# One paced stream of modulation sums, shorter inversion steps, and an earlier start of the z jobs, in a one-layer hybrid block

## The chip, the cores and the metric

The kernel runs on one core of a Trainium2 chip. The metric is the device time of one execution in microseconds (us). Three executions of the kernel before took 1974.28, 1973.03 and 1969.95 us; the median is 1973.03.

## What is computed

One layer for one batch of T = 256 tokens with D = 2048 channels, everything in float32:

```python
mod = silu(c) @ W_ada + b_ada      # 6 x 2048 numbers: shift/scale/gate for the mixer and for the FFN
h = rms_norm(x) * (1 + scale_m) + shift_m
proj = h @ W_in                    # mLSTM q,k,v,o and gates; GDN q,k,v, z, beta, decay; merge gates
y_a = (sigmoid(a_o) * norm(bidirectional mLSTM, 4 heads)) @ W_a
o_b = bidirectional gated delta rule, 16 heads, chunks of 64
      # each chunk: T = inverse(I + beta * k k^T * decay, strictly lower), u = T (beta v), w = T (beta exp(g) k)
y_b = (norm(o_b) * silu(z)) @ W_b
x = x + gate_m * ((g_a * y_a + g_b * y_b) @ W_out)
x = x + gate_f * (silu(gate) * up) @ W_down      # FFN of width 5632 on the normed, modulated x
return rms_norm(x)
```

## The kernel before

**Matmuls.** Every large product is made in split precision: a raw weight tile (1 MB) is loaded on SP's DMA queue into `raw`, ScalarE (ACT) copies half of it into the high part `wh` (line 213, or 182 for the narrow jobs), VectorE (DVE) subtracts to get the low part `wl` (line 215, or 184), and TensorE (PE) makes three products: high times high, high times low, low times high (lines 234 to 236). `raw`, `wh` and `wl` have three buffers each. Half a raw tile is a *half chunk*: 12 matmuls of 512 columns in `tjob`, 24 of 256 columns in `fjob`. A job of `tjob` is 8 half chunks for 512 output columns. The loop body makes the split of a half chunk and then its matmuls; with the argument `early` = n, the first n splits are made at the first `next` of the job, before its PSUM tiles are taken, and all splits of the job keep the written order (`order`). What is not given to `order` is placed by a scheduler that may move it among its neighbours on the same engine.

**Stages.** The projections of x with the modulation's first two parts come first, then the gated delta rule (GDN) in four groups of four heads, g = 0 to 3; then `y_b`, mLSTM, `y_a`, the output jobs `o`, and the FFN (gate, up, down), which takes from about 1260 us to the end. In the GDN stage the chain of small steps leaves TensorE free, so a stock of filling jobs `rest` (the mLSTM projections v, o, a and the merge gates mb, ma) is run between them: `fill(n)` runs n half chunks of the first job in `fills`.

**One GDN group.** `invert(g)` runs `gdn_invert(g)`, which inverts the 64 small triangles of the group's chunks by 30 rank-one updates on VectorE, two instructions each (the `utmp` and `uu` operations, line 704 on). It begins after a load of the triangles from DRAM (`uu` from `inst_d`). It yields whenever the size of the updates since the last yield is over 720, and at each yield `invert` runs one half chunk. Ahead of it, `invert` runs 4 half chunks (6 for g = 0). The inverted blocks go through DRAM and come back in `gdn_blocks(g)`; `fill(8)` stands between its first two steps. Then the loop over two pairs of heads, p = 0 and 1, with n = 1 to 9, interleaves three things: the steps of `gdn_phase2(g, p)` (matmuls p1 to p4, pa, pb, pc, po, then the norm, the transposes px), the next group's narrow jobs `b` and their heads' `gdn_phase1` (through `stream`), and fills. In `gdn_phase1` the products `ks` are turned into the tiles mi, mb, gg and at by ten VectorE operations and a transpose. At the end of groups 0 to 2 the next group's z job (`z_job(g + 1)`, 8 half chunks) is put in front of the fills, and `invert(g + 1)` runs. In group 3 two mLSTM heads (`first2`) are started beside the GDN.

**Modulation sums.** Parts 2, 3 and 4 of the modulation (48 vectors of 128), and part 5 in the FFN, are not made on TensorE. For each vector `ask()` loads 1 MB of W_ada on SP's queue, and `add()` multiplies it by silu(c) and sums it in one VectorE instruction (line 124, 2.28 us each). `pump()` is called once per half chunk and paces them: `every` says after how many half chunks a sum is owed, `held` forbids a sum, `age` counts half chunks since the load was asked. `room` holds the pool, the tag, the number of buffers and the number of loads asked at once.

```python
elif asked:
    if owed[0] and age[0] > 2 and not held[0]:
        owed[0] = 0
        add()
elif unasked and every[0]:
    ask()
```

The pace before: `every` is 1 in the loop over p and n; it is 0 in the inversions and in the z jobs, and from the end of group 3 to the end of the first mLSTM heads; it is 1 again for mLSTM heads 2 and 3; for the `y_a` jobs `room` is changed to three buffers of the pool "sr" and `every` is 4; in the `o` jobs `sums()` is called at fixed places, and `sums(P)` finishes all that are left at step 4 of the last one.

Of the kernel before, what the change touches and what calls it, by code (L numbers as in the profile page):

```python
# [9 lines left out]
F32 = mybir.dt.float32  # L10
# [5 lines left out]
P = 128  # L16
T = 256
D = 2048
# [34 lines left out]
def hybrid_block(ctx: ExitStack, tc: tile.TileContext, xr, nfr, crow, pk_d, cst_d, ada2, ada4, win0, winb, wint, wba, wbb, wo, wgu, wd, out, dbg=None):  # L53
# [3 lines left out]
    def pool(stack, name, bufs=1, **kw):  # L57
        return stack.enter_context(tc.tile_pool(name=name, bufs=bufs, **kw))
# [3 lines left out]
    rows_p = pool(ctx, "rows")  # L62
# [9 lines left out]
    def order(ins, yes=True):  # L72

        return tc.keep_in_program_order(ins) if yes else ins
# [30 lines left out]
        order(S.activation(row_c[:, g * 512 : (g + 1) * 512], pc_, AF.Silu))  # L105


    room = [(rows_p, "ada", 1, 1)]
    asked, unasked, age = [], [], [0]

    def ask():

        pl, tag, bufs, _ = room[0]
        part, b = unasked.pop(0)
        raw = pl.tile([P, D], F32, tag=tag, bufs=bufs, name=f"ada{part}_{b}")
        order(nc.sync.dma_start(raw, ada4[part - 2, b]))
        asked.append((part, b, raw))
        age[0] = 0

    def add():  # L120

        part, b, raw = asked.pop(0)
        c = part * KB + b
        order(V.scalar_tensor_tensor(raw, raw, 1.0, row_c[:, :D], ALU.mult, ALU.mult, accum_out=mod[:, c : c + 1]))  # L124
        if b == KB - 1:
            c = slice(part * KB, part * KB + KB)
            V.tensor_tensor(mod[:, c], mod[:, c], pk[:, PK_ADAB + c.start : PK_ADAB + c.stop], ALU.add)
# [16 lines left out]
            f()  # L144

    count, every = [0], [0]
    owed, held = [0], [False]

    def sums(n=1):

        while n and (unasked or asked):
            while unasked and len(asked) < room[0][3]:
                ask()
            add()
            n -= 1

    def pump():
        count[0] += 1
        age[0] += 1
        if every[0] and count[0] % every[0] == 0:  # L160
            owed[0] = 1
        if room[0][3] > 1:
            if owed[0]:
                owed[0] = 0
                sums()
        elif asked:
            if owed[0] and age[0] > 2 and not held[0]:
                owed[0] = 0
                add()
        elif unasked and every[0]:  # L170
            ask()

    def fjob(name, src, done):
# [93 lines left out]
    fills = []  # L267

    def fill(n=1):

        while n and fills:
            if next(fills[0], None):
                n -= 1
            else:
                fills.pop(0)
# [90 lines left out]
    def z_job(g, early=0):  # L366
        def done(ps):
            szs[g] = evp.tile([P, 2, 512], F32, tag="sz", bufs=1, name=f"sz{g}")
            for t in range(2):
                S.activation(szs[g][:, t], ps[t], AF.Silu)  # L370
        return tjob(f"z{g}", [wint[g, u] for u in range(4)], hh, hl, done, early)
# [121 lines left out]
    with ExitStack() as s0:  # L493
# [18 lines left out]
        def loads(b):  # L512
            ra = [w0.tile([P, D + 2], F32, tag="ra", bufs=5, name=f"ra{b}_{i}") for i in range(2)]
            raw = st.tile([P, N0, P], F32, tag="raw", bufs=3, name=f"raw0_{b}")
            for i in range(2):
                order(nc.sync.dma_start(ra[i], ada2[b, :, i]))
            order(nc.sync.dma_start(raw, win0[b]))
            return ra, raw
# [10 lines left out]
        ra, raw = loads(0)  # L529
# [18 lines left out]
        for b in range(KB):  # L548
            if b:
                ra, raw = loads(b)  # L550
# [15 lines left out]
        zj = z_job(0, 3)  # L566
# [121 lines left out]
    def gdn_invert(g):  # L688

        uu = uus.pop(g)  # L690
        tmp = bk.tile([64, 256], F32, tag="utmp", bufs=1, name=f"utmp{g}")
        inv = inv_d[g].rearrange("j b (x h) i -> h (b x) j i", h=GRP)

        def store(rows):
            for e in range(GRP):
                G.dma_start(inv[e, :, rows], uu[16 * e : 16 * e + 16, rows])

        yield
        order(V.memset(uu.rearrange("p j i -> p (j i)")[:, ::33], 1.0))
        size = 0  # L700
        for i in range(30, 0, -1):
            w = 31 - i
            t3 = tmp[:, 0 : i * w].rearrange("p (j c) -> p j c", j=i)
            order(V.tensor_tensor(
                t3,
                uu[:, 0:i, i : i + 1].broadcast_to([64, i, w]),
                uu[:, i : i + 1, i + 1 :].broadcast_to([64, i, w]),
                ALU.mult,
            ))
            order(V.tensor_tensor(uu[:, 0:i, i + 1 :], uu[:, 0:i, i + 1 :], t3, ALU.add))  # L710
            if i == 16:
                store(slice(16, 32))
            size += i * w + 125
            if size > 720:
                size = 0
                yield
        store(slice(0, 16))
# [165 lines left out]
    def drive(gen, n=2):  # L883
        for _ in gen:
            fill(n)
# [132 lines left out]
    def invert(g):  # L1018
        gen = gdn_invert(g)
        next(gen)  # L1020
        fill(4 if g else 6)
        for _ in gen:
            fill(1)

    invert(0)
    for g in range(4):
        blocks = gdn_blocks(g)
        next(blocks)
        fill(8)
        next(blocks)  # L1030
        fill(1)
        pairs = [gdn_phase2(g, p) for p in range(2)]
        if g == 3:
            settle()
            sf.close()
            mq["pool"] = pool(sq_, "mq", side="right")
            first2 = [mlstm(h) for h in range(2)]
            for c in first2:
                next(c)
        every[0] = 1  # L1040
        for p in range(2):
            pieces = stream(4 * g + 2 * p + 4)
            for n in range(1, 10):

                held[0] = n < 4
                if p == 0:
                    next(blocks, None)
                next(pairs[p], None)
                if g == 3 and n == (8, 4)[p]:
                    next(first2[p])  # L1050
                for _ in range(last[n] if g == 3 else second[n] if p else after[n]):
                    next(pieces)
            for _ in pairs[p]:
                pass

            if g < 3:
                while 4 * g + 2 * p + 5 not in heads:
                    next(pieces)
        if g < 3:
            fills.insert(0, z_job(g + 1))  # L1060
            every[0] = owed[0] = 0
            invert(g + 1)
    settle()
    sx.close()
# [53 lines left out]
            yield from y_b(g)  # L1118

    o4s = [o_load(g) for g in range(2)]  # L1120
    every[0] = owed[0] = 0
    cores = steps(*first2)
    fill(1)
    next(cores)
# [19 lines left out]
    o_split(3, o4s[3])  # L1144
    fill(2)
    drive(cores, 3)
    every[0] = 1
    drive(steps(mlstm(2), mlstm(3)), 3)
    fill(1000)
    mgh, mgl = big(bigC, F32R, "mgh"), big(bigC, F32R, "mgl")  # L1150
    sm_.close()
    sr_ = ExitStack()
    if asked:
        add()
    room[0] = (pool(sr_, "sr"), "sr", 3, 3)
    gm = room[0][0].tile([P, D], F32, name="gm")
    dgs = {}

    def row_diag(part, g, rp):
        ms = mods[:, part == 5]  # L1160
        if not g:
            m = mod[:, part * KB : (part + 1) * KB]
            V.tensor_copy(ms[:, 0], m)
            V.tensor_tensor(ms[:, 1], m, ms[:, 0].bitcast(F32), ALU.subtract)
        dg = dgs[part, g] = rp.tile([P, 2, 4, P], F32R, tag="dg", bufs=2, name=f"dg{part}_{g}")
        for i in range(2):
            V.tensor_tensor(
                dg[:, i], ident.unsqueeze(1).broadcast_to([P, 4, P]),
                ms[:, i, 4 * g : 4 * g + 4].bitcast(F32).unsqueeze(2).broadcast_to([P, 4, P]), ALU.mult,
            )  # L1170
# [6 lines left out]
            PE.matmul(pr, onesr, woven(dg[:, i]), start=i == 0, stop=i == 1)  # L1177
        S.activation(woven(dst[:, g * 512 : (g + 1) * 512]), pr.rearrange("p (c h) -> p c h", h=2), AF.Copy)

    every[0] = 4  # L1180
    for g in range(4):
        for i, _ in enumerate(y_a(g)):
            if g and i == 3:
                merged(g - 1, mgh, mgl)
            if i in (1, 5) and g < 2:
                row_diag(2, 2 * g + i // 4, room[0][0])
            if i in (3, 7) and g < 2:
                row_spread(2, 2 * g + i // 4, gm)
    every[0] = 0


    def o_job(g, front=None):
# [26 lines left out]
    def root():  # L1219

        order(S.activation(rs1[:, 2:3], ones1, AF.Sqrt))
# [83 lines left out]
    for g in range(4):  # L1305
        if g == 3:
            root()
        for i, _ in enumerate(o_job(g, front_o if g == 3 else None) if g else o_first, 0 if g else 2):
            if i in ((4, 7), (2, 5), (2, 5), (0, 2))[g]:
                sums()  # L1310
            if g == 3 and i == 4:
                sums(P)
                V.scalar_tensor_tensor(
                    affn, mod[:, 4 * KB : 5 * KB], 1.0, pk[:, PK_NFFN : PK_NFFN + KB], ALU.add, ALU.mult
                )
    if dbg is not None and "x1" in dbg:
        G.dma_start(dbg["x1"], x1)
    room[0] = (rows_p, "ada", 1, 1)
    ada_parts(5)
    sw.close()  # L1320
    sr_.close()
# [73 lines left out]
    for j in range(FB // 4):  # L1395
# [4 lines left out]
        for e2 in range(2):  # L1400
            px = gps(f"pxf{j}_{e2}")
            for e in range(2):
                f = 2 * e2 + e
                for t in range(2):
                    PE.transpose(px[:, e * T + t * P : e * T + (t + 1) * P], sg[:, t, f * P : (f + 1) * P], ident)
            b = 4 * j + 2 * e2
# [156 lines left out]
```

## Time and profile before

| | |
|---|---|
| runs | 1974.28, 1973.03, 1969.95 us; median 1973.03 |
| profiled execution | 1974.3 us; span from first to last instruction 1972.4 us |
| mean granted TensorE clock | 0.994 |
| busy | PE 98%, weight loads (PEld) 86%, DVE 71%, ACT 52%, POOL 6% |
| memory | 467.07 MB read, 16.82 MB written, 245 GB/s over the span |

Everything in the profile belongs to one execution. "Busy" is the share of the span in which the engine ran an instruction; PE and PEld overlap. "PEclk" is the granted TensorE clock, 1.00 at full speed. In a list of operations each line has the start (us from the start of the span), the duration in us, the engine, the line of the kernel, the operation, the tiles out<-in with their shapes, and, in brackets, the wait before it and what ended it.

### The profile page before, as it was taken

To read this page: it belongs to the slowest core of one execution; us is meant where nothing else is said; L and a number is where in the kernel's file an instruction comes from. 1 tells how busy PE (TensorE), PEld (TensorE's weight loads), DVE (VectorE), ACT (ScalarE), POOL (GpSimd) and SP (SyncE) were. 2 spreads that over 40 slices of the span, in tenths; PEclk is the share of its full clock that TensorE was granted. 3 is DMA by queue.
4 is the path that set the end of the run, shared out by engine and by line. 5 is a ranking of instruction groups with operands and counts; after the bars stand their busy time and mean duration, and the time that the engine had idled before them with its cause. 6 is when DMAs were issued, how large, how long until landed. Compare 5 with 4: busy or idle time off the path is not lost.

```text
span 1972.4 us, 27079 instructions
## 1 busy us (share of the span) xinstructions
PE 1929.4 (98%) x10418; PEld 1703.5 (86%) x10418; DVE 1405.5 (71%) x2067; ACT 1030.0 (52%) x1555; POOL 116.5 (6%) x211
## 2 busy tenths in 40 slices
PE   8999999999999999999999999999999999999998
PEld 6878889998998899889787888888888888888886
DVE  6779887887888798866577878866665665555554
ACT  3137656764766577565544444644444444444444
POOL 0001210111001010110100000200000000000000
PEclk9999999999999999999999999999999999999999
DMA  9987676766566666586777888566676665565663
GB/s 399 420 349 226 184 249 240 252 214 208 203 217 213 237 218 229 192 296 246 277 282 266 323 317 330 191 252 238 238 265 241 237 238 205 197 213 197 208 199 142
DMA packets 78962, 485.64 MB, mean 246 GB/s; under 512 B 10585, under 2 KB 15969, under 8 KB 24433
## 3 DMA queue, kind: packets, MB, share of 16 engines
q1 hardware_dynamic: 63216, 450.69, 62.9%
q0 software_dynamic: 8160, 17.88, 4.5%
q10 hardware_dynamic: 7458, 15.36, 2.1%
q8 instruction: 81, 1.33, 0.3%
q14 instruction: 47, 0.39, 0.1%
HBM read 467.07 MB, written 16.82 MB: 245 GB/s over the span
## 4 chain that ended last, share of the span: by engine, by line
PE 81%; DVE 8%; DMA 6%; ACT 2%; issue 1%; POOL 0%; ACTq 0%; SPq 0%; DVEq 0%; POOLq 0%
PE acc_gt L234 4%; PE acc_gt L235 4%; PE acc_gt L236 4%; PE acc_up L236 4%; PE acc_up L235 4%; PE acc_up L234 4%; PE acc_d L236 4%; PE acc_d L235 4%; PE acc_d L234 4%; DMA ra<-ada 3%; PE acc_b L187 2%; PE acc_b L188 2%; PE acc_b L189 2%; PE acc_o L236 2%; PE acc_o L234 2%; PE acc_o L235 2%
## 5 line engine op out<-in xcount | busy, mean ns | idle before, releaser
L215 DVE TENSOR_TENSOR wl_d<-raw_d,wh_d 128x1024 fp32r<-128x1024 f32 x88 | 107.7, 1224 | 105.9 <-ACT wh_d L213 105.9
L215 DVE TENSOR_TENSOR wl_up<-raw_up,wh_up 128x1024 fp32r<-128x1024 f32 x88 | 107.7, 1224 | 100.2 <-ACT wh_up L213 100.1
L215 DVE TENSOR_TENSOR wl_gt<-raw_gt,wh_gt 128x1024 fp32r<-128x1024 f32 x88 | 108.1, 1229 | 80.2 <-ACT wh_gt L213 80.2
L187 PE MATMUL acc_b<-hh,wh_b 128*128 128x256 f32 x576 | 163.0, 283 | 0.6 <-ACT wh_b L182 0.6
L189 PE MATMUL acc_b<-hh,wl_b 128*128 128x256 f32 x576 | 159.6, 277 | 0.8 <-DVE wl_b L184 0.8
L188 PE MATMUL acc_b<-hl,wh_b 128*128 128x256 f32 x576 | 159.2, 276 | 0.0
L213 ACT ACTIVATE wh_d<-raw_d 128x1024 fp32r<-128x1024 f32 x88 | 92.9, 1056 | 126.5 <-PE acc_d L235 117.7
L213 ACT ACTIVATE wh_gt<-raw_gt 128x1024 fp32r<-128x1024 f32 x88 | 92.9, 1056 | 118.6 <-PE acc_gt L235 71.1
L213 ACT ACTIVATE wh_up<-raw_up 128x1024 fp32r<-128x1024 f32 x88 | 92.8, 1055 | 108.1 <-PE acc_up L235 77.1
L124 DVE SCALAR_TENSOR_TENSOR ada<-ada,crow 128x2048 f32<-128x2048 f32 x64 | 146.0, 2284 | 0.0
L234 PE MATMUL acc_gt<-wh_gt,hfh 128*128 128x512 f32 x352 | 135.6, 385 | 0.6 <-ACT hfh L1350 0.6
L235 PE MATMUL acc_gt<-wh_gt,hfl 128*128 128x512 f32 x352 | 134.9, 383 | 0.0
L236 PE MATMUL acc_gt<-wl_gt,hfh 128*128 128x512 f32 x352 | 134.1, 381 | 0.0
L234 PE MATMUL acc_up<-wh_up,hfh 128*128 128x512 f32 x352 | 133.4, 379 | 0.0
L235 PE MATMUL acc_up<-wh_up,hfl 128*128 128x512 f32 x352 | 133.4, 379 | 0.0
L236 PE MATMUL acc_up<-wl_up,hfh 128*128 128x512 f32 x352 | 133.4, 379 | 0.0
L234 PE MATMUL acc_d<-wh_d,ffh 128*128 128x512 f32 x344 | 130.5, 379 | 0.0
L235 PE MATMUL acc_d<-wh_d,ffl 128*128 128x512 f32 x344 | 130.5, 379 | 0.0
L236 PE MATMUL acc_d<-wl_d,ffh 128*128 128x512 f32 x344 | 130.4, 379 | 0.0
L561 PE MATMUL first<-x,raw 128*128 128x256 f32 x512 | 114.5, 382 | 7.2 <-ACT x L555 7.2
L561 PEld LDWEIGHTS first<-x,raw 128*128 128x128 f32 x512 | 96.0, 190 | 25.7 <-ACT x L555 13.3
L189 PEld LDWEIGHTS acc_b<-hh,wl_b 128*128 128x128 f32 x576 | 111.3, 193 | 1.0 <-DVE wl_b L184 1.0
(383 smaller groups left out, 5263.1 us busy)
## 6 DMA issues: line engine op xcount, KB each, us to landing
ada<-ada SPq DMA_DIRECT2D x64, 1024.0 KB, 6.0
raw_gt<-wgu SPq DMA_DIRECT2D x44, 1024.0 KB, 4.9
raw_up<-wgu SPq DMA_DIRECT2D x44, 1024.0 KB, 4.9
raw_d<-wd SPq DMA_DIRECT2D x44, 1024.0 KB, 4.9
raw_b<-winb SPq DMA_DIRECT2D x36, 1024.0 KB, 5.3
ra<-ada SPq DMA_DIRECT2D x32, 1025.0 KB, 15.8
raw<-win SPq DMA_DIRECT2D x16, 1024.0 KB, 14.5
raw_z<-wint SPq DMA_DIRECT2D x16, 1024.0 KB, 5.0
```

The costliest lines, as they stand in the source:

```text
L124: order(V.scalar_tensor_tensor(raw, raw, 1.0, row_c[:, :D], ALU.mult, ALU.mult, accum_out=mod[:, c : c + 1]))
L187: PE.matmul(o, wh[:, k], woven(hh[:, kk]), start=kk == 0, stop=False)
L188: PE.matmul(o, wh[:, k], woven(hl[:, kk]), start=False, stop=False)
L189: PE.matmul(o, wl[:, k], woven(hh[:, kk]), start=False, stop=kk == KB - 1)
L213: order(S.activation(wh, raws[u][:, k0 : k0 + 2], AF.Copy), early)
L215: order(V.tensor_tensor(wl, raws[u][:, k0 : k0 + 2], wh.bitcast(F32), ALU.subtract), early)
L234: order(PE.matmul(ps[t], xh[:, kk, c], woven(wh[:, k]), start=kk == 0, stop=False), early and steps > 1)
L235: PE.matmul(ps[t], xl[:, kk, c], woven(wh[:, k]), start=False, stop=False)
L236: PE.matmul(ps[t], xh[:, kk, c], woven(wl[:, k]), start=False, stop=kk == last)
L561: PE.matmul(first[o], raw[:, o], x[:, b], start=b == 0 and o % 2 == 0, stop=b == KB - 1 and o % 2 == 1)
```

## The change

- `room` goes: a sum always has the one buffer "ada", so one load is under way at a time, from the GDN stage to the FFN.
- A new bound `calm`: a new load is asked for only when `age` has reached it. It is 1 at first, 3 in the loop over p and n of groups 0 to 2, and 1 again from the inversion on. `age` is set to 0 by `ask` and now also by a sum.
- `every` is set to 1 once per group, right after the first step of `gdn_blocks(g)` and so ahead of `fill(8)`, and stays 1 through `y_b`, mLSTM, `y_a` and `o`, until step 3 of the last `o` job, where `sums(P)` now stands. In `invert(1)` to `invert(3)` it is 0 as before. The fixed `sums()` calls in the `o` jobs go, and so does the pace of 4 in `y_a`.
- `gdn_invert` yields when the size is over 580 instead of 720: 13 yields in the updates instead of 10, and one half chunk is run at each.
- The z job of group g + 1 is created with `early` = 1 at p = 1, n = 9, and its first split is made there, ahead of that step of `gdn_phase2` and of what is left of the stream; the same job is then put in front of the fills.

The FFN and the amount of work are unchanged.

```diff
-    room = [(rows_p, "ada", 1, 1)]
...
     def ask():
-        pl, tag, bufs, _ = room[0]
         part, b = unasked.pop(0)
-        raw = pl.tile([P, D], F32, tag=tag, bufs=bufs, name=f"ada{part}_{b}")
+        raw = rows_p.tile([P, D], F32, tag="ada", name=f"ada{part}_{b}")
...
-    owed, held = [0], [False]
+    owed, held, calm = [0], [False], [1]
     def sums(n=1):
         while n and (unasked or asked):
-            while unasked and len(asked) < room[0][3]:
+            if not asked:
                 ask()
...
     def pump():
...
-        if room[0][3] > 1:
-            if owed[0]:
-                owed[0] = 0
-                sums()
-        elif asked:
+        if asked:
             if owed[0] and age[0] > 2 and not held[0]:
-                owed[0] = 0
+                owed[0] = age[0] = 0
                 add()
-        elif unasked and every[0]:
+        elif unasked and every[0] and age[0] >= calm[0]:
             ask()
...
-            if size > 720:
+            if size > 580:
                 size = 0
                 yield
...
         next(blocks)
+        every[0], held[0] = 1, False
         fill(8)
...
-        every[0] = 1
+        calm[0] = 3 if g < 3 else 1
         for p in range(2):
...
                     next(blocks, None)
+                if g < 3 and p and n == 9:
+                    zj = z_job(g + 1, 1)
+                    next(zj)
                 next(pairs[p], None)
...
-            fills.insert(0, z_job(g + 1))
+            fills.insert(0, zj)
             every[0] = owed[0] = 0
+            calm[0] = 1
             invert(g + 1)
...
-    every[0] = owed[0] = 0
+    held[0] = False
     cores = steps(*first2)
...
-    every[0] = 1
     drive(steps(mlstm(2), mlstm(3)), 3)
...
-    if asked:
-        add()
-    room[0] = (pool(sr_, "sr"), "sr", 3, 3)
-    gm = room[0][0].tile([P, D], F32, name="gm")
+    sr = pool(sr_, "sr")
+    gm = sr.tile([P, D], F32, name="gm")
...
-    every[0] = 4
     for g in range(4):
         for i, _ in enumerate(y_a(g)):
...
-    every[0] = 0
...
         for i, _ in enumerate(o_job(g, front_o if g == 3 else None) if g else o_first, 0 if g else 2):
-            if i in ((4, 7), (2, 5), (2, 5), (0, 2))[g]:
-                sums()
-            if g == 3 and i == 4:
+            if g == 3 and i == 3:
+                every[0] = owed[0] = 0
                 sums(P)
```

More of the change, by code (lines that the diff above doesn't have):

```diff
@@ L1185, in hybrid_block @@
             if i in (1, 5) and g < 2:
-                row_diag(2, 2 * g + i // 4, room[0][0])
+                row_diag(2, 2 * g + i // 4, sr)
             if i in (3, 7) and g < 2:
                 row_spread(2, 2 * g + i // 4, gm)
-    every[0] = 0
     def o_job(g, front=None):
@@ L1317, in hybrid_block @@
         G.dma_start(dbg["x1"], x1)
-    room[0] = (rows_p, "ada", 1, 1)
     ada_parts(5)
```

## The prediction, made before the change was run

> **What bounds the kernel now.** I read the page first, then who TensorE waited for, then busy time by stretch, then the timeline at the places that the change moves.
>
> ```profile
> span 1972.4 us, 27079 instructions
> PE 1929.4 (98%) x10418; PEld 1703.5 (86%) x10418; DVE 1405.5 (71%) x2067; ACT 1030.0 (52%) x1555; POOL 116.5 (6%) x211
> ```
>
> TensorE (PE) is busy for 1929.4 of 1972.4 us. The change leaves every matmul in place, so all that it can win or lose is in the 43 us of idle time and in the clock. Who ended that idle time:
>
> ```profile
> engine line waited for: us in total, times, longest us
> PE acc_ya L236 <- DVE wl_ya L215: 3.8, 2, 2.2
> PE acc_z L234 <- ACT wh_z L213: 2.5, 1, 2.5
> PE p L770 <- DVE pt L762: 1.0, 1, 1.0
> ```
>
> The same by stretch; the columns are us, then busy time of PE, PEld, DVE, ACT and POOL, then PEclk, DMA share and GB/s:
>
> ```profile
> 430.00:480.00 50.00, 48.24 (x223) 41.62 (x222) 42.98 (x91) 25.86 (x32) 7.94 (x15) 1.00 0.67 215
> 480.00:500.00 20.00, 17.71 (x138) 16.74 (x137) 10.31 (x14) 11.00 (x18) 1.99 (x4) 1.00 0.47 162
> 614.00:660.00 46.00, 44.23 (x204) 38.05 (x203) 40.88 (x87) 23.78 (x30) 7.96 (x15) 1.00 0.67 209
> 790.00:840.00 50.00, 47.23 (x282) 42.28 (x281) 43.17 (x91) 25.79 (x34) 7.14 (x13) 0.97 0.61 199
> 900.00:1000.00 100.00, 99.95 (x593) 86.92 (x592) 62.72 (x86) 56.42 (x97) 9.33 (x15) 1.00 0.77 278
> 1080.00:1104.00 24.00, 20.19 (x85) 16.72 (x84) 19.34 (x22) 9.25 (x9) 0.00 (x0) 0.93 0.97 368
> 1400.00:1500.00 100.00, 100.00 (x471) 87.01 (x471) 61.61 (x56) 45.24 (x48) 0.00 (x0) 1.00 0.69 249
> 793.20:796.60 3.40, 3.15 (x7) 2.06 (x8) 1.77 (x2) 3.32 (x9) 2.05 (x4) 0.51 0.12 20
> 581.60:585.00 3.40, 3.40 (x18) 3.40 (x18) 2.42 (x8) 2.31 (x5) 0.00 (x0) 0.51 1.00 412
> 1025.30:1028.70 3.40, 3.40 (x10) 2.68 (x9) 1.24 (x3) 0.00 (x0) 0.00 (x0) 0.51 0.87 265
> 1086.80:1090.20 3.40, 3.40 (x9) 2.63 (x8) 3.20 (x4) 1.19 (x2) 0.00 (x0) 0.50 0.97 301
> ```
>
> Rows one, three and four are the inversions of head groups 1, 2 and 3 with their z jobs: 1.8, 1.8 and 2.8 us idle. Row two is the wait for group 1's inverted blocks, 2.3 us. Row six is the start of the y_a jobs, 3.8 us, with DMA at 0.97: there three modulation sums and their loads come in one burst. Row five says that the end of group 3 and the mLSTM beside it have no idle time today. Row seven gives the unit: 471 matmuls in 100 us, so a half chunk (12 of them) is 2.6 us of TensorE. The last four rows are stretches of 3.4 us at half clock; each costs 3.4 x 0.5 = 1.7 us.
>
> **What the change takes away.** One sum per four half chunks from one buffer replaces the burst at y_a: 3.8 us and the half clock behind it (1086.80), 5.5 us. It moves sums, and makes none new, so VectorE's (DVE's) total stays. On SP's queue each sum's load is now one of every three or four transfers with the weights behind it. The load waits for its single buffer, thus for the sum before it; in the changed queue that sum stands ahead of the split that frees the next weight buffer, so I cost it at nothing.
>
> Smaller inversion chunks make 13 instead of 10 steps between which one half chunk of filling work goes. That gives three more half chunks, 7.8 us, for the trip of the blocks through DRAM: I count the 2.3 us at 480 to 500 as gone. The inversion's own waits (1.8, 1.8 and 2.8 us, the last with the half clock at 793.20, 1.7 us) I take out and put their new size in below. Taken out in all: 5.5 + 2.3 + 1.8 + 1.8 + 4.5 = 15.9 us.
>
> **What it adds at the z jobs.** Passing early=1 splits the first pair ahead, but it also makes every split of the job keep its program order. In the queues of the changed kernel the first wl of z1, z2 and z3 now stands behind the whole mi/mb/at chain of the last head, while the matmuls of ks and px stand right ahead of the z job. For z1 and z2 that is new. Here is z2 today (VectorE, TensorE, then ScalarE):
>
> ```profile
> 607.94 1.22 DVE L215 TENSOR_TENSOR wl_z<-raw_z,wh_z 128x1024 fp32r<-128x1024 f32 x1
> ...
> 612.18 0.35 DVE L647 SCALAR_TENSOR_TENSOR mi<-ks,sm,dec 128x128 f32<-128x128 f32 x1 [1.00 <-PE ks L642]
> ...
> 615.04 1.18 DVE L215 TENSOR_TENSOR wl_z<-raw_z,wh_z 128x1024 fp32r<-128x1024 f32 x1
> 616.14 0.68 DVE L594 TENSOR_TENSOR_SCAN dec<-al,cst 128x256 f32<-128x256 f32 x1
> ```
>
> ```profile
> 612.98 0.46 PE L234 MATMUL acc_z<-wh_z,hh 128*128 128x512 f32 x1
> ```
>
> ```profile
> 616.35 1.06 ACT L213 ACTIVATE wh_z<-raw_z 128x1024 fp32r<-128x1024 f32 x1
> ```
>
> ```profile
> 624.52 0.20 DVE L704 TENSOR_TENSOR utmp<-uu 64x30 f32<-64x30 f32 x1 [1.39 <-DMA uu<-inst_d]
> ```
>
> Today the first wl_z is done at 609.2, before the chain. After the change it takes the place at 615.04 and is done at 616.2. TensorE begins z2 at 612.98, has four matmuls that need only wh (0.9 us), and then waits from 613.9 to 616.2: 2.3 us. For z3 the chain is the same and the hole 2.1 us. Three holes: 6.7 us.
>
> Then the inversion. Today two more splits of z (the third chunk's) run before its first operation; in the changed queue eight inversion operations stand ahead of them, and these wait for the DMA that lands at 624.5. Eight operations at 0.2 to 0.3 us take 2.1 us, the split 1.15 us: wl at 627.8. TensorE, which by then has done four half chunks (to 626.0) wants it at 626.4: 1.4 us. The next split has six operations (2.0 us) ahead of it and is done at 630.9, wanted at 630.3: 0.6 us. From there VectorE gives 1.15 us of split and 1.5 to 1.7 us of inversion per half chunk of 2.6 us, so it is late by 0.1 to 0.3 us each time, together about 0.9 us. So 2.9 us for z1 and for z2; for z3, which has no decay load and no dec scans in between, half, 1.5 us. Sum 7.3 us. The lower bound of this term is zero (the DMA lands some 3 us earlier), the upper the double.
>
> Does a hole bring a half clock? The quoted rows show one after a hole of 2.5 us (793.20) and of 2.2 us (1086.80), and one each at 581.60 and 1025.30, where only small matmuls had run. I take one in two for the three z holes: 3 x 0.5 x 1.7 = 2.6 us. [...]
>
> **What it adds at the end of group 3.** The three extra fills of each inversion come out of a fixed stock. In the changed queue the stock ends early: its last half chunk (ma3's) stands ahead of po of the last pair, and nothing stands between po and px. Today three half chunks do:
>
> ```profile
> 938.22 0.39 PE L834 MATMUL po<-z,at 128*128 128x128 f32 x2
> ...
> 946.22 0.60 PE L841 MATMUL px<-cst,on 128*128 128x128 f32 x4
> ```
>
> ```profile
> 938.09 2.28 DVE L124 SCALAR_TENSOR_TENSOR ada<-ada,crow 128x2048 f32<-128x2048 f32 x1
> ...
> 941.84 1.13 DVE L868 SCALAR_TENSOR_TENSOR on<-po,so,sz 128x128 f32<-128x128 f32 x4
> ```
>
> ```profile
> 939.81 1.28 ACT L862 ACT_TABLE_LOAD   x1
> 941.10 0.30 ACT L862 ACTIVATE so<-so,epsc 128x4 f32<-128x4 f32 x1
> ```
>
> po ends at 938.6 and the last "on" at 943.0, whatever TensorE does: 4.4 us of bare chain, as a sum stands ahead of it on VectorE in both queues. Behind it come 24 one-column matmuls (pden), so 1.5 half-clock stretches, 2.6 us. Sum 7.0 us; bounds 3 and 10.
>
> **At the boundary of group 0.** In the changed queue the splits of b6 fall behind the chain of head 5, as the eviction of ma0 with its own table loads comes ahead of nn5. Today:
>
> ```profile
> 366.41 1.19 DVE L184 TENSOR_TENSOR wl_b<-raw_b,wh_b 128x1024 fp32r<-128x1024 f32 x1
> ...
> 374.04 0.65 DVE L762 TENSOR_TENSOR pt<-p,cst 128x512 f32<-128x512 f32 x1
> ```
>
> The split that is done by 367.6 today is done at 375.8, behind pt; TensorE has four matmuls from 372.9 on, then waits for pt at 374.7: 1.3 us, and half a half clock, 0.8 us. Sum 2.1 us.
>
> **The sum.** Added: 6.7 + 7.3 + 2.6 + 7.0 + 2.1 = 25.7. Taken away: 15.9. The half clocks at 581.60 and 1025.30 hang on where small matmuls fall and recur about half the time: another 1.7 off. Net +8.1 us on the profiled execution (1974.3 us; its span is 1972.4). That execution is 1.3 us above the median of 1973.03, so the forecast is 1981.
>
> **Rivals.** First, *faster*: the holes at z cost only what VectorE is really short of. If the inversion's DMA lands by about 621 instead of 624.5 (z3's earlier chain speaks for that), the 7.3 us go; if the tail's hole is covered but for 3 us and no z hole meets a half clock, 25.7 becomes 6.7 + 3 + 1.3 = 11.0, and the net is 11.0 - 15.9 = -4.9 us: about 1968. It decides from the point where the added waits stay under 12 us. Against it stands the queue order, which no landing changes. Second, *no change*: the same terms, each a little smaller (z inversion 3 instead of 7.3, one half clock in the tail): +2 us, 1975. The same 1975 comes out if no new hole halves the clock (2.6 + 2.6 + 0.8 = 6.0 off); the rows at 793.20 and 1086.80 speak against it. Third, *more*: every new hole brings its half clock (another 4.3 us) and the sums that now run during the eight fills behind each inversion hold up the splits by the 0.6 us seen above, six times: +16 us, 1989. Row five's VectorE at 63% speaks against the last.
>
> **How the numbers follow.** Forecast 0.45; third rival 0.15; no change 0.2; faster 0.2. What can be told from no change is 0.2%, 3.9 us, so 1969.1 to 1977.0 is "same": faster 0.2, same 0.2, slower 0.6. The range goes from the faster rival's 1968 to 1990, just over the third's.
>
> **What would show it.** In the new trace: TensorE waiting for wl_z three times, 2 us each, just behind px; no wait for wl_ya; no idle at the p matmuls of group 1; a hole of 4 to 5 us ahead of the last px, with PEclk at 0.5 behind it. The prediction is wrong if wl_z is not among the longest waits of TensorE, or if 900 to 1000 stays as full as it is.

## The result, and the profile after

The changed kernel took 1997.73 us (median of four runs, 1993.29 to 1998.56) against 1972.8 us (median of four, the three given above and one of 1972.57): a ratio of 1.0125, 95% interval 1.0107 to 1.0144. It is 24.9 us slower; 8 us had been forecast, with 1990 as the upper end of the range. The profiled execution has a span of 1995.0 us against 1972.4.

The totals and the waits of TensorE, from the page of the changed kernel and its view of waits:

```profile
span 1995.0 us, 27075 instructions
PE 1936.0 (97%) x10418; PEld 1706.3 (86%) x10418; DVE 1404.5 (70%) x2067; ACT 1025.7 (51%) x1551; POOL 116.8 (6%) x211
```

```profile
PE acc_z L230 <- DVE wl_z L209: 15.7, 10, 3.8
PE acc_o L230 <- DVE wl_o L209: 5.0, 2, 2.5
PE acc_a L183 <- DVE wl_a L178: 4.2, 1, 4.2
PE px L835 <- DVE on L862: 4.0, 1, 4.0
PE p L764 <- DVE pt L756: 1.2, 1, 1.2
```

As many matmuls, as many DVE instructions; the wait for wl_ya is gone, and in its place stand wl_z, px, and two that the forecast does not have: wl_a and wl_o, 9.2 us.

A table by stage tells where it went. "Lost" is, over all TensorE instructions of a stage, the time from one start to the next less the median for instructions of that kind: idle time and slow clock together. It adds up to the span's difference. The row of group 3 holds the wait ahead of the last px too.

| stage | lost before, us | lost after, us | difference |
|---|---|---|---|
| start to the end of inversion 0 | 14.2 | 13.3 | -0.9 |
| group 0 | 1.3 | 2.4 | +1.1 |
| z1, inversion, blocks, group 1 | 9.3 | 13.5 | +4.2 |
| z2, inversion, blocks, group 2 | 4.2 | 17.0 | +12.8 |
| z3, inversion, blocks, group 3 | 5.3 | 17.3 | +12.0 |
| y_b, mLSTM | 2.2 | 2.7 | +0.5 |
| y_a | 6.0 | -0.1 | -6.1 |
| o | 0.5 | -0.1 | -0.6 |
| FFN | 7.9 | 7.7 | -0.2 |

The same by stretch (us, then busy time of PE, PEld, DVE, ACT, POOL, then PEclk, DMA share, GB/s). First the z jobs with their inversions, the start of y_a, and stretches at half clock:

```profile
434.90:484.90 50.00, 46.73 (x215) 39.38 (x213) 45.81 (x95) 26.96 (x33) 6.55 (x13) 1.00 0.64 204
627.60:677.60 50.00, 43.57 (x191) 36.25 (x190) 41.41 (x89) 24.85 (x31) 5.75 (x11) 0.97 0.58 195
823.90:873.90 50.00, 45.22 (x209) 38.38 (x207) 42.64 (x88) 26.15 (x33) 4.94 (x9) 1.00 0.56 190
1107.00:1131.00 24.00, 24.00 (x113) 21.02 (x112) 20.47 (x23) 11.51 (x11) 0.00 (x0) 1.00 0.88 318
504.80:511.60 6.80, 5.02 (x24) 5.02 (x25) 6.17 (x7) 4.85 (x10) 0.00 (x0) 0.51 0.30 77
630.90:634.30 3.40, 3.37 (x8) 2.74 (x9) 3.40 (x5) 1.63 (x3) 2.18 (x4) 0.51 0.22 34
702.40:705.80 3.40, 3.40 (x9) 2.71 (x10) 3.40 (x4) 1.02 (x2) 0.00 (x0) 0.54 0.79 246
985.80:992.60 6.80, 6.80 (x26) 5.25 (x26) 0.59 (x6) 1.76 (x5) 1.10 (x2) 0.51 0.51 187
```

Idle time in the three inversions is 3.3, 6.4 and 4.8 us (before: 1.8, 1.8, 2.8). At y_a there is none, and DMA is at 0.88 instead of 0.97.

Then the trips of the inverted blocks through DRAM, from the last inversion operation (uu) to the transpose of the loaded blocks (cg). Before, then after, each for groups 1 to 3:

```profile
474.80:489.70 14.90, 14.90 (x97) 13.77 (x96) 6.05 (x6) 5.20 (x6) 4.21 (x8) 1.00 0.83 278
657.20:670.50 13.30, 13.30 (x63) 11.66 (x63) 7.13 (x6) 6.07 (x7) 4.22 (x8) 1.00 0.79 271
832.80:848.00 15.20, 15.20 (x72) 13.29 (x72) 8.39 (x7) 6.51 (x7) 8.40 (x15) 1.00 0.80 255
```

```profile
483.80:503.10 19.30, 18.60 (x157) 18.14 (x155) 9.31 (x8) 7.39 (x10) 4.23 (x8) 1.00 0.99 372
681.10:699.30 18.20, 18.20 (x86) 15.95 (x85) 9.43 (x9) 7.88 (x9) 4.23 (x8) 1.00 0.95 343
874.30:892.10 17.80, 17.80 (x84) 15.56 (x83) 9.36 (x10) 5.69 (x6) 7.97 (x15) 1.00 1.01 364
```

The trip takes 2.6 to 4.9 us longer, and the DMA share during it is 0.95 to 1.01 instead of 0.79 to 0.83. How that reaches TensorE is seen in the timeline of VectorE at the end of group 1's trip:

```profile
503.14 0.71 DVE L719 STREAM_TRANSPOSE cg<-cg 128x512 f32<-128x512 f32 x1 [6.76 <-DMA cg<-inv_d]
503.77 0.31 DVE L723 TENSOR_SCALAR R<-cg,cst 128x256 f32<-128x256 f32 x1
504.12 0.48 DVE L724 SCALAR_TENSOR_TENSOR R<-cg,cst,R 128x256 f32<-128x256 f32 x1
504.52 0.35 DVE L723 TENSOR_SCALAR R<-cg,cst 128x256 f32<-128x256 f32 x1
504.90 0.48 DVE L724 SCALAR_TENSOR_TENSOR R<-cg,cst,R 128x256 f32<-128x256 f32 x1
505.31 1.22 DVE L178 TENSOR_TENSOR wl_a<-raw_a,wh_a 128x1024 fp32r<-128x1024 f32 x1
```

The transpose waits 6.76 us for the blocks, and a split wl_a that has nothing to do with them stands behind it in VectorE's queue. Its high part wh_a had been ready since 497.8, yet VectorE starts nothing while it waits; TensorE, idle since 502.4, gets wl_a at 506.58. So the wait carries the name of a weight, not of the blocks. In groups 2 and 3 the transpose waits 5.60 and 5.68 us (for group 3 the profile names another load, bc), and a split wl_o stands behind it whose wh_o had been ready since 695.1 and 887.7.

### The profile page after: what moved, and what is told of

Read it like the earlier page. It is cut to its first block, busy times and chain, and to the rows that moved or that the text cites. A ratio compares the mean times of both kernels' runs of the same rounds, so it can differ in the third digit from the quotient of the medians.

```text
span 1995.0 us, 27075 instructions
## 1 busy us (share of the span) xinstructions
PE 1936.0 (97%) x10418; PEld 1706.3 (86%) x10418; DVE 1404.5 (70%) x2067; ACT 1025.7 (51%) x1551; POOL 116.8 (6%) x211
## 5 line engine op out<-in xcount | busy, mean ns | idle before, releaser
L182 PEld LDWEIGHTS acc_b<-hl,wh_b 128*128 128x128 f32 x576 | 110.6, 192 | 0.1
## 6 DMA issues: line engine op xcount, KB each, us to landing
ra<-ada SPq DMA_DIRECT2D x32, 1025.0 KB, 15.2
```

The costliest lines, as they stand in the source:

```text
L182: PE.matmul(o, wh[:, k], woven(hl[:, kk]), start=False, stop=False)
```

## The experiments

Ratios are to the kernel before in the same set of runs, which is 1973.4 to 1975.4 us there; the changed kernel stands at 1.0125.

A difference in microseconds depends by up to 3.3 us on how it is taken. For a variant of the changed kernel it is the median's distance from 1997.73, which comes from another set of runs; by the ratios the five that are faster gain 0.7 to 2.5 us more. For a variant of the kernel before it goes by the ratio; in the two cases where the medians of the set are more than 2 us away, both are given.

**1. The trip without sums.** The changed kernel, with the pace set behind the fills:

```diff
-        every[0], held[0] = 1, False
         fill(8)
         next(blocks)
         fill(1)
+        every[0], held[0] = 1, False
```

> The changed kernel with the modulation sums held off, as before, until the inverted blocks are back from DRAM (the pace set to 1 behind the eight fills and the one after them, not ahead of them). Theory: the 1 MB loads of the sums fill the DMA engines (share 0.95 to 1.01 during the trip, against 0.79 to 0.83 before) and lengthen the trip from 13.3-15.2 to 17.8-19.3 us; without them the trip is 15.5 us or less in groups 1 to 3, TensorE's waits for wl_a and wl_o behind it (4.2 + 2.5 + 2.5 us) fall under 3 us in all, their half clocks go, and the time is 9 to 14 us under the changed kernel's: 1984 to 1989 us. Rival (the smaller inversion chunks shift the trip against its cover): the waits stay and the time is within 3 us of the changed kernel's 1997.7.

Measured: 2023.89 us, ratio 1.0251 (1.0231 to 1.0271), so the expected time is missed by far. Behind the trips (15.6 to 16.2 us) the waits for wl_a and wl_o were gone, as the theory has it, but a hole of 38.9 us opened ahead of the FFN. The groups of VectorE between 1265 and 1312 us show why:

```profile
L122 DVE SCALAR_TENSOR_TENSOR ada<-ada,crow 128x2048 f32<-128x2048 f32 x7 | 16.0, 2293 | 26.4 <-DMA ada<-ada 26.4
```

Seven sums had not been made when the FFN needed them, and ran one by one behind their loads from the single buffer. With `calm` at 3 and no sums in the trip only 18 of 48 were made before the y_b jobs (24 in the kernel before, 29 in the changed one). So the next run gives them a place:

> As the first trial with the sums held off until the blocks are back, but with calm at 1 in the loop, so that the sums not made during the trip are made in the loop and none is left over for the last o job. Theory: the trip of the blocks is 15.5 us or less in groups 1 to 3, the waits behind it (4.2 + 2.5 + 2.5 us in the changed kernel, with about 5 us of half clock) come to 3 us or less, there is no hole at the start of the FFN beyond the 3.1 us of all other kernels, and the time is about 12 us under the changed kernel's 1997.7: 1986 us. Rival (the sums were better placed in the trip than in the loop, where they hold up the splits of the b jobs): waits of 8 us or more turn up in the loop, and the time is 1994 or more.

Here `calm` is 1 in the loop too. Measured: 1985.84 us, ratio 1.0059 (1.0044 to 1.0074), as forecast. The trips are 15.6, 15.7 and 16.9 us, the last 1.4 us over the forecast's 15.5, at a DMA share of 0.83 to 0.84, and no wait stands behind them. One sum is still left over (24 were made before y_b): its load adds 3.5 us to the wait for xn ahead of the FFN.

**2. The loads or the sums?** The changed kernel; sums asked for in the eight fills get no load and read `row_c` instead, so that it computes other numbers:

```diff
+        if not quiet[0]:
             order(nc.sync.dma_start(raw, ada4[part - 2, b]))
```

> The changed kernel, but sums that are asked for during the eight fills behind an inversion get no load: they run on data that lie in the chip, so the same VectorE instructions are there and about two loads of 1 MB per group are left out (eight of the sums are then of other data). Theory (the DMA engines): the trip is 15.5 us or less and the waits for wl_a and wl_o behind it fall from 9.2 us to 3 us or less; about 10 us under the changed kernel's 1997.7: 1987 us. Rival (VectorE: the sums of 2.28 us each stand ahead of the blocks' transposes or of the split behind them): the trip stays at 17 us or more and the time within 3 us of 1997.7.

Measured: 1986.02 us, ratio 1.0062 (1.0047 to 1.0077). The trips:

```profile
484.80:498.20 13.40, 13.40 (x113) 13.13 (x112) 9.27 (x9) 6.52 (x9) 4.21 (x8) 1.00 0.88 296
676.90:693.30 16.40, 16.40 (x78) 14.36 (x77) 9.43 (x10) 7.74 (x9) 4.22 (x8) 1.00 0.74 251
865.70:879.90 14.20, 14.20 (x67) 12.43 (x67) 9.35 (x10) 5.67 (x6) 7.99 (x15) 1.00 0.78 264
```

VectorE is as busy in them as in the changed kernel (9.3 to 9.4 us), yet the waits are gone. It is the loads. They also show in the transfers of the blocks themselves. From issue to landing the four loads of a trip take 6.7 to 7.9 us in the changed kernel (medians of the three trips), 4.2 to 4.6 here and 2.6 to 4.2 in the kernel before; the four stores take 5.7 to 6.6, 4.2 to 4.8 and 4.5 to 5.7. The second trip, 16.4 us, is over the 15.5 of the expectation: its last two stores take 6.2 and 6.6 us to land, against 3.8 to 4.2 in the other two trips, and why is open.

**3. Sums in the trip alone.** The kernel before, with the pace set ahead of `fill(8)`:

> The kernel before with the pace of the sums set to 1 ahead of the eight fills behind each inversion, so that sums run during the trip of the blocks, and nothing else. Theory: the DMA share in the trip rises from 0.8 to 0.95 or more, the trip from 13.4-15.2 to 16.5 us or more in groups 1 to 3, and TensorE's waits behind it from 2.3 to 7 us or more in all: with their half clocks 5 to 10 us, ratio 1.0025 to 1.005. Rival (the trip is hidden in this kernel, where it starts earlier against its cover, and the sums made there relieve the burst at y_a): ratio 1.000 or less.

Measured: 2000.31 us, ratio 1.0139 (1.0119 to 1.0159): this line alone costs about as much as the whole change, 27 us by the ratio and 25 by the medians, and not the 5 to 10 expected. The waits for the blocks' R, and the trips of groups 1 and 2:

```profile
PE p L761 <- DVE R L730: 14.2, 2, 7.6
```

```profile
479.60:497.90 18.30, 13.31 (x102) 12.61 (x100) 8.32 (x8) 6.55 (x8) 4.21 (x8) 0.94 0.96 339
671.10:689.30 18.20, 13.07 (x72) 11.57 (x70) 8.20 (x9) 6.26 (x7) 4.22 (x8) 0.93 0.93 348
```

TensorE runs dry after 13 us and is idle for 5 us within each trip; the mean granted clock over the two trips is 0.94 and 0.93.

**4. The smaller inversion chunks.** Taken out of the changed kernel (`size > 720`):

> The changed kernel with the inversion's bound at 720 again (10 steps instead of 13). Theory: the fills that the extra steps took are there again at the end of group 3, so that the wait ahead of the last px (4.0 us) and the two half-clock stretches behind it (3.4 us) go, and the time is about 7 us under the changed kernel's 1997.7: 1990 us; the first z holes of 2.2 us and the long trip stay. Rival one (the smaller chunks also set the trip's length or cover): 9 us or more beyond that, 1981 or less. Rival two (without the smaller chunks VectorE gives the splits even later): the waits in the inversion grow by more than is won at the end, and the time is 1997 or more.

Measured: 1993.61 us, ratio 1.0092 (1.0068 to 1.0116), 4 us better instead of 7 (6.5 by the ratios). The wait ahead of the last px is gone, as forecast; but 6.9 us of waits for R came, behind trips that are no longer than with the chunks. The other way round, put alone into the kernel before (`size > 580`):

> The kernel before with the inversion's bound at 580 alone. Theory: the three more half chunks per inversion come out of the stock, so the wait ahead of the last px (4 us) with two half-clock stretches (3.4 us) appears, and the trip of the blocks is as long as before (15.5 us or less) with the same 2.3 us behind it in group 1: 4 to 7 us, ratio 1.002 to 1.0035. Rival (the steps give VectorE's splits their place, and the waits of 0.8 to 1 us in the inversions go): ratio 1.000 or less.

Measured: 1974.21 us, ratio 0.9999 (0.9988 to 1.0009). The tail's hole is there (3.6 us, with 10.2 us at half clock from 959.5 on), but the trips of 14.0 to 14.8 us have no wait behind them any more, z3's wait for wh_z (2.5 us) does not appear, and it comes out even. And together with sums in the trip:

> The kernel before with sums in the trip (1.0139 alone) and the smaller inversion chunks (0.9999 alone). Theory (the three half chunks more make TensorE come later to the matmuls that need the blocks, so they cover part of the longer trip): the waits behind the trips, 6.6 and 7.6 us in groups 1 and 2 with sums alone, fall to 2 to 5 us each as in the changed kernel, and the ratio is 1.006 to 1.010. Rival (they do not act on each other): the waits stay at 6 us or more and the ratio at 1.0135 or more.

Measured: 1984.46 us, ratio 1.0057 (1.0039 to 1.0075), just under the expected range. The trips are as long (18.3, 16.6, 16.9 us), the waits are 5.0, 2.7 and 2.8 us. Group 1's inversion ends at 486.5 us and TensorE runs dry at 503.3: 16.8 us of cover against 13.3 with sums alone. So the three half chunks lengthen the cover by 3.5 us, not by the 7.8 us that they last: the inversion itself ends 6.9 us later (486.5 against 479.6). That is enough for a trip of 14.8 us, and not for one of 18.3.

**5. The early z job.** Taken out of the changed kernel:

```diff
-                if g < 3 and p and n == 9:
-                    zj = z_job(g + 1, 1)
-                    next(zj)
-            fills.insert(0, zj)
+            fills.insert(0, z_job(g + 1))
```

> The changed kernel with the z jobs made where they were before and without early=1. Theory: the fixed order of the z splits costs the three first holes (2.2 us each, 6.5 in all) and most of the later ones in the inversion (1.1 + 3.8 + 2.4 us), with one half clock of 1.7 us; what comes back is the kernel before's late first split of z3 (2.5 us and a half clock) and small waits (about 3 us). Net 7 to 9 us under the changed kernel's 1997.7: about 1990 us, with no wl_z wait of TensorE over 1.2 us. Rival (the splits are late because VectorE has too much to do in 13 short steps, whatever their order): waits for wl_z, or for the fills behind it, stay at 10 us or more and the time is within 3 us of 1997.7.

Measured: 1986.2 us, ratio 1.0054 (1.0039 to 1.007): 11.5 us better (14.0 by the ratios), above the range given. Of the waits for wl_z 1.5 us is left, that of the first z job. Put alone into the kernel before:

> The kernel before with the early z job alone (early=1 at p = 1, n = 9 of groups 0 to 2). Theory (additive): it costs here what its removal won from the changed kernel, 11.5 us: three first holes of 2.2 us for wl_z, later ones in the inversions, and a half clock or two; ratio to the kernel before 1.004 to 1.007. Rival (the holes come only together with the smaller inversion chunks, which put more inversion operations ahead of the splits): 1.002 or less, with holes in the inversions under 2 us in all.

Measured: 1983.47 us, ratio 1.0058 (1.0038 to 1.0079): 11.4 us by the ratio, 8.1 by the medians, with 14.4 us of waits for wl_z in all. The rival, that it takes the smaller chunks, is out. With the early split but without the bound order (`order(..., early > 1)` at both splits):

> The changed kernel with the same early first split of the z jobs, but their splits not bound to the written order (that binding is kept for the first z job and the gate job). In the queue, the first two wl_z of each z job then stand ahead of the mi/mb/at chain, and the third chunk's ahead of the inversion. Theory (the binding costs it, not the early split): the three first holes of 2.2 us go, the later ones for wl_z (7.5 us) fall under 3 us, one half clock less, and the kernel before's late z3 split does not come back: 12 to 14 us under 1997.7, about 1985 us. Rival (VectorE is short in the inversion whatever the order): the waits move to the fills behind the z job, and the time is within 4 us of 1997.7.

Measured: 1988.87 us, ratio 1.0073 (1.0058 to 1.0088), 9 us better rather than 13 (10.3 by the ratios). The three first holes are gone and so, but for one, are the waits in the inversion; one of 2.9 us in inversion 2 stays. So most of the cost is the binding; the early split by itself does not beat the late one (1986.2).

**6. The pace from y_b on.** Put alone into the kernel before, `every` 1 from the end of group 3 and one buffer:

> The kernel before with the new pace of the sums only from the end of group 3 on: one buffer, a sum asked for and made at every third or fourth half chunk through the y_b, mLSTM, y_a and o jobs, the rest at step 3 of the last o job. Theory: the burst at the start of y_a goes with its waits for wl_ya (3.8 us) and its half clock (1.7 us), and nothing takes its place: 5.5 us under the kernel before, ratio 0.9972. Rival: the loads, spread among the weights of y_b and the mLSTM chain, make other weights late, and the ratio is 0.999 or more.

Measured: 1969.9 us, ratio 0.9975 (0.9963 to 0.9986), as forecast. This part is a gain. Three versions built on it:

> The kernel before with the new pace from the end of group 3 on (0.9975 of the kernel before when run alone), and z3's first split made early, without the bound order. Theory: TensorE's wait for the first wh_z of z3 (2.5 us, as ScalarE copies it behind the obt evictions) goes with its half clock of 1.7 us or more: ratio to the kernel before about 0.9955. Rival: what is saved there comes back as a later px eviction or a later split in the inversion, and the ratio stays at 0.9975.

Measured: 1971.69 us, ratio 0.9988 (0.9979 to 0.9998): no further gain. The wait for wh_z falls from 2.5 to 0.5 us, and one of 1.5 us for wl_z follows 2.6 us later, with another of 1.8 us (for wl_a) in the inversion.

> The kernel before with the new pace from the end of group 3 on, and nine half chunks instead of eight behind the inversion of group 1. Theory: the trip of group 1 (14.9 us) misses its cover by 2.3 us; one more half chunk (2.6 us) covers it, and the half clock that followed at 581.6 may go too; two of the three half chunks between the last po and px are left, which still cover most of that chain: 2 to 4 us under the kernel with the new pace alone, ratio to the kernel before about 0.996. Rival: the missing half chunk opens a hole of 2 to 3 us ahead of the last px, and the ratio stays at 0.9975.

Measured: 1968.65 us, ratio 0.9971 (0.9958 to 0.9985). The waits behind group 1's trip shrink from 2.3 us to one of 1.3 us; from the version without the ninth half chunk it cannot be told apart. It is the fastest of all that were run, and it beats both kernels.

> The changed kernel's new pace from the end of group 3 on and its smaller inversion chunks, without sums in the trip and without the early z jobs. Theory (the sums in the trip, 11.9 us, and the early z jobs, 11.5 us, are together what the change loses): what is left is 1997.7 - 11.9 - 11.5 = 1974 by subtraction, 1969 by adding the single gains to the kernel before (b_cad 0.9975, 580 alone 0.9999); ratio 0.997 to 1.000. Rival (something else of the change costs 5 us or more, with the smaller chunks in the new pace): ratio 1.0025 or more.

Measured: 1974.3 us, ratio 1.0003 (0.9993 to 1.0013). The change without its two costly parts (and without `calm`) is level with the kernel before, so nothing else of size is lost in it. But the gain of the new pace does not come on top: as in the trial with `calm` at 1, 24 sums were made before y_b instead of the 25 with the new pace alone, the last sum ends late, and the wait for xn ahead of the FFN is 5.3 us instead of 1.6.

## Why the prediction was wrong

The direction was right, the size was not: +8.1 us was forecast, +24.9 came. The signs that the prediction names came to the letter, also the one for the term that failed: TensorE has no wait at the p matmuls of group 1, but at the same place it loses 4.18 us to wl_a. The working, term by term:

- **The burst at y_a, 5.5 us off.** Right: alone it gives 5 us, and the rows at 1107 show no idle time.
- **The first z holes, 6.7 us.** Right in size, place and cause. TensorE's timeline at z2 shows the four matmuls on wh and then the hole, 2.18 us as in the other two:

```profile
628.37 0.38 PE L229 MATMUL acc_z<-wh_z,hl 128*128 128x512 f32 x1
630.93 1.19 PE L230 MATMUL acc_z<-wl_z,hh 128*128 128x512 f32 x2 [2.18 <-DVE wl_z L209]
```

- **The z splits in the inversion, 7.3 us.** The largest three holes are 0.9, 3.75 and 2.4 us, 7.0 us; z1 was put too high, z2 and z3 too low. One half clock, 1.7 us, followed where 2.6 us had been put. With what the forecast takes out of the inversions (1.8 + 1.8 + 4.5) its z part is +8.5 us; the two experiments on it show 8.1 and 11.5 by the medians, 11.4 and 14.0 by the ratios, so it was right in kind and perhaps a little low.
- **The tail of group 3, 7.0 us.** Right: 3.97 us and two half-clock stretches, 7.4 us.
- **The boundary of group 0, 2.1 us.** The wait for pt came at 1.2 us, without a half clock.
- **The half clocks at 581.60 and 1025.30, 1.7 us off.** One of the two came again, at 1054.25. The one at 581.60 had been read as following small matmuls only; a wait of 1.39 us for vf ended at 580.27 as well. That the two hang on where small matmuls fall, and recur half the time, was the author's estimate; no run shows it.
- **The step that failed: "I count the 2.3 us at 480 to 500 as gone", with the sums' loads costed "at nothing".** The first half holds where no sums run there: with the smaller chunks alone the wait is gone. But the 2.3 us were not a wait for the blocks themselves, as they were read. They are waits for wh_b (0.56), wl_b (0.77) and pt (0.95); the matmuls on the blocks' R ran from 491.79 without a wait. And the cover of 7.8 us is 3.5 us in the one pair of runs that shows it. The second half is wrong. The change also starts sums during the eight fills, and their loads were looked at only on SP's queue, against the weights behind them. The store and the load of the inverted blocks are issued by GpSimd on another queue, but they count into the same DMA share, which was 0.8 in the trip before (in group 1's trip GpSimd's queue had 8.6 of the 83%, SP's 64.9), and they landed later once the sums' loads ran beside them (experiment 2). The trips took 13.3 to 15.2 us at a share of 0.79 to 0.83 and 17.8 to 19.3 us at 0.95 to 1.01. Whether the DMA engines or the memory behind them set the pace, no run tells apart. The cost is 9.2 us of waits and half clocks at 505 and 702, together 11.9 us by one experiment and 11.7 by the other (13.0 and 12.4 by the ratios).
- **The rival that named the sums in the fills** had them hold up splits on VectorE by 0.6 us each, 3.6 us in all. The place was right, the mechanism was not: with the same VectorE work and no loads the cost is gone.

The forecast's 8.1 us and these 11.9 make 20.0 of the 22.6 us between the two spans. The last 2.6 us lie within what single executions of one kernel differ by (1993.29 to 1998.56), and no run assigns them. The parts do not simply add: the sums in the trip cost 25 to 27 us alone, 10 to 11 us on top of the smaller chunks and 12 to 13 us inside the change.

## What to carry to other kernels

The round trip through DRAM took 13.3 to 15.2 us here at a DMA share of 0.79 to 0.83 and 17.8 to 19.3 us at 0.95 to 1.01, though the loads that were added are issued on SP's queue and the trip's transfers on GpSimd's. So before other transfers are moved into the cover of such a trip, its length must be worked out at the DMA share that will then hold, and that share counts every queue. A wait with the name of a weight may be a wait for something queued ahead of it on the same engine (here 4.18 us for wl_a, whose split stood behind a transpose that waited 6.76 us for the blocks), so the row above the releaser has to be read too. And work that is paced in the background has a deadline: count how much of it each stage takes in, because what is left over is paid at the latency of its loads (26.4 us for the seven sums of the first trial, 3.5 us for the one of the second).

## What the runs showed of the hardware

In the changed kernel's trace the half clock did not go by the length of a hole. Stretches that begin at the end of a hole of 3.75 us (646.6) and of 2.53 us (895.0) run at full clock, while those after 2.18 us (630.9) and 2.45 us (702.4), shown above, run at half:

```profile
646.60:650.00 3.40, 3.19 (x14) 2.50 (x15) 3.19 (x9) 1.06 (x1) 0.00 (x0) 1.00 0.00 0
895.00:898.40 3.40, 3.40 (x20) 3.07 (x20) 3.40 (x4) 3.32 (x7) 0.00 (x0) 1.00 0.92 327
```

Nor did holes of one length agree. The first holes of z1 and z3 are of 2.18 us too, and behind them the clock stays full:

```profile
438.20:441.60 3.40, 3.40 (x16) 3.00 (x17) 3.40 (x5) 2.60 (x3) 1.66 (x4) 1.00 0.28 43
827.20:830.60 3.40, 3.40 (x16) 3.00 (x17) 2.73 (x3) 2.64 (x3) 1.30 (x3) 1.00 0.36 55
```

And one half clock came without a hole. The half-clock stretches between 300 and 1250 us begin at 504.70, 631.00, 702.68, 985.98 and 1054.25 and last 6.8, 3.4, 3.4, 6.8 and 3.4 us. Ahead of the last of them TensorE has no idle time for 3.4 us, of which the 24 one-column matmuls of pden take 2.73 from 1051.54 on:

```profile
1050.80:1054.20 3.40, 3.40 (x30) 3.29 (x28) 2.81 (x5) 1.23 (x2) 0.00 (x0) 1.00 0.92 383
1054.30:1057.70 3.40, 3.40 (x9) 2.67 (x10) 1.52 (x5) 0.17 (x1) 0.00 (x0) 0.51 0.92 295
```

This is a reading of one trace, and no run was made to test it. What decides whether a hole is followed by half clock is not shown. The forecast's one in two for the three z holes was an estimate, and one of the three was followed by half clock.
